# The first chunk of x transposed tile by tile ahead of its norm in a macaron decoder step

## The chip, the cores and the metric

One NeuronCore of a Trainium2 chip runs the whole program; the other cores are idle. The metric is the device time of one execution in microseconds (us). Five engines work side by side, each through its own list of instructions in a fixed order: TensorE (PE in the profile, with its weight loads listed as PEld), VectorE (DVE), ScalarE (ACT), GpSimd (POOL) and SyncE (SP), which here only issues DMAs. An engine whose next instruction waits for a semaphore runs nothing that stands behind it.

## The reference, cut to what matters

The program computes one step of a hybrid recurrent decoder with one layer, for 1024 prompt rows and 32 sample rows of width 1024. The change is in the first half-step, which is a SwiGLU feed-forward block on normalised rows:

```python
def rmsnorm(x, g):
    xf = x.astype(jnp.float32)
    y = xf * lax.rsqrt(jnp.mean(xf * xf, axis=-1, keepdims=True) + EPS)
    return (y * g.astype(jnp.float32)).astype(x.dtype)

def swiglu(x, w_gu, w_down):
    gate, up = jnp.split(x @ w_gu, 2, axis=-1)
    return (jax.nn.silu(gate) * up) @ w_down
...
x = x + 0.5 * swiglu(rmsnorm(x, norm_ffn1[l]), w_ffn1_gu[l], w_ffn1_down[l])
```

A mixer (three kinds of heads behind one input projection) and a second SwiGLU block follow, and a last RMSNorm. The change leaves all of that alone.

## The kernel before, in words

x arrives in nine tiles of 128 rows, in three chunks of three tiles (`CH`: 384, 384 and 288 columns once transposed). The kernel keeps x transposed: `xT[k]` holds columns 128k to 128k+127 of x on the partitions, with the rows of x along the free dimension. A chunk is brought in by `x_chunk(c)`. First `rms_rows` takes the sum of squares of each tile (tiles 0 and 2 on ScalarE, tile 1 on VectorE), one square root (ScalarE), one reciprocal and three scaled identities `dg` (VectorE); three products of `dg` with a matrix of ones (TensorE, "row products" below) spread the reciprocal norms over all partitions, and ScalarE copies them to `F1.row`. Then 24 TensorE transposes (three tiles by eight k) go through PSUM, and ScalarE and VectorE copy the eight results into `xT[k]`, every other one each.

All float32 products are made of three fp32r products: a matrix is split into a high part `h` (a cast on ScalarE) and a low part `l` (a subtraction on VectorE), and each k contributes l·xh, h·xl and h·xh. `raw1(j)` loads the gate and up columns of weight block j, `parts` splits them. `F1.build(0, first=True)` makes the normalised x in blocks: for each k one VectorE product of `xT[k]`, the gain and `row` (`b`), one ScalarE cast (`fh`) and one VectorE subtraction (`fl`); `b11` and `b21` are the first quarter of the rows (264 columns, k 0 to 3 and 4 to 7), `b12` and `b22` the second quarter.

`plain(j, q, ...)` computes block j for quarter q: 24 products for the gate (`pg`), a Silu on ScalarE, 24 products for up (`pu`), a VectorE product `z` and a store. The program text runs `plain(0,0)`, `x_chunk(1)`, `plain(1,0)`, `plain(2,0)`, `x_chunk(2)`, then the small vectors of the later stages (`small_vectors(8, ...)`: nine small loads into `vr`, one transpose, one copy), then `plain` for quarter 1 of blocks 0, 1, 2 and for blocks 20 and 21, and then the long `gate_up` loop, whose first product in the profile is `pb` at L430.

The order on each engine is set by a scheduler, which places the instructions by priorities and by its own idea of durations; `tc.keep_in_program_order` pins an instruction to its place among the other pinned ones. Before the change the squares and the other steps of `rms_rows` are pinned for chunks 1 and 2, and the transposes are pinned nowhere. `AHEAD`, `AHEAD_GU` and `AHEAD_EV` raise priorities. The scheduler opens two PSUM tags of four banks here, "mm" and "aux". The lines that are spoken of:

```python
r0 = raw1(0)
x_chunk(0)
W = {0: [parts(r) for r in r0]}
...
next(b0)
next(b0)
W[1] = [parts(r, pin=tc.keep_in_program_order) for r in r1]
plain(0, 0, W[0], F1, hd1)
x_chunk(1)
plain(1, 0, W[1], F1, hd1)
```

Of the kernel before, what the change touches and what calls it, by code (L numbers as in the profile page):

```python
# [15 lines left out]
AF = mybir.ActivationFunctionType  # L16
# [14 lines left out]
CH = [(0, 384), (384, 384), (768, 288)]  # L31
# [57 lines left out]
def build(ctx, tc, I, O, cdP, cd4):  # L89
    nc = tc.nc  # L90
    pe, act, dve, gps, sp = nc.tensor, nc.scalar, nc.vector, nc.gpsimd, nc.sync
# [17 lines left out]
    def B(name, dt=F32):  # L109
        return blk.tile([P, PITCH], dt, name=name, tag="b")[:, :BW]  # L110

    def ps2(name):
        return pool["pp"].tile([P, 2, 512], F32, name=name, tag="two")

    def ps(tag="aux", name="ps"):
        if pool["gu"]:
            return ps2(name)[:, 0, :]
        return pool["pp"].tile([P, 512], F32, name=name, tag=tag)

    def tm(name, tag, n=384, bufs=None):  # L120
# [8 lines left out]
    idt = cst.tile([P, P], F32, name="idt")  # L129
    make_identity(nc, idt)  # L130
    ones = cst.tile([P, P], F32, name="ones")
    dve.memset(ones, 1.0)
    epsb = cst.tile([P, 1], F32, name="epsb")
# [6 lines left out]
    def tr(out, in_):  # L140
        k = in_.shape[0]
        return pe.transpose(out, in_, idt[:k, :k])


    sm = cst.tile([P, 64], F32, name="sm")
    SMO = {}

    def small_vectors(o, names):
        vr = tm("vr", "sq", P)
        gps.memset(vr, 0.0)  # L150
        n = 0
        for name in names:
            a = I[name]
            src = a.rearrange(("(k p) -> k p", "l (k p) -> (l k) p", "l j (k p) -> (l j k) p")[len(a.shape) - 1], p=P)
            sp.dma_start(vr[n:n + src.shape[0], :], src)
            SMO[name] = o + n
            n += src.shape[0]
        p = ps()
        tr(p[:, :P], vr)
        dve.tensor_copy(sm[:, o:o + n], p[:, :n])  # L160

    def col(name, i):
        return sm[:, SMO[name] + i:SMO[name] + i + 1]
# [7 lines left out]
    def wtile(tag, k, m, dt=F32R):  # L171
        t = ws.tile([P, KT * P], dt, name=tag, tag=tag)
        return t[:, :k * m].rearrange("p (k m) -> p k m", k=k)

    def raw(srcs, nk, m, pin=lambda i: i):
        r = wtile("wr", nk, m, F32)
        k0 = 0
        for s in srcs:
            n = s.shape[0] // P
            pin(sp.dma_start(r[:, k0:k0 + n, :], s.rearrange("(k p) m -> p k m", p=P)))  # L180
            k0 += n
        return r

    def parts(r, e=dve, home=None, pin=lambda i: i):
        h, l = home() if home else (wtile("wh", *r.shape[1:]), wtile("wl", *r.shape[1:]))
        pin(act.copy(h, r))  # L186
        tt(l, r, h, SUB, e)
        return h, l
# [21 lines left out]
    def rel(c, i):  # L210
        return tok(3 * c + i) - CH[c][0]


    def tiles(c):
        return [(i, rel(c, i)) for i in ((0, 1, 2) if c < 2 else (2, 0, 1))]
# [178 lines left out]
    def plain_weights(wgu, j):  # L394
        with tc.high_priority(AHEAD_GU):
            return [parts(raw([wgu[:, o + j * P:o + (j + 1) * P]], KT, P)) for o in (0, FF)]

    def plain(j, q, W, F, hd, step=lambda: None):

        X = [F.f[i, 0] for i in ((0, 1) if q == 0 else (7, 5))]  # L400

        def product(p, u):
            h, l = u
            for k in range(KT):
                xh, xl = (x[:, k % 4] for x in X[k // 4])
                pe.matmul(p, l[:, k], xh, start=k == 0, stop=False)
                pe.matmul(p, h[:, k], xl, start=False, stop=False)
                pe.matmul(p, h[:, k], xh, start=False, stop=k == KT - 1)
            step()

        g, u, z = ps("mm", "pg")[:, :Q], ps("aux", "pu")[:, :Q], tm("z", "s")[:, :Q]
        product(g, W[0])
        with tc.high_priority(AHEAD_EV):
            act.activation(z, g, AF.Silu)
        product(u, W[1])
        with tc.high_priority(AHEAD_EV):
            stt(z, u, 0.5, z, MUL, MUL)
        sp.dma_start(hd[j * P:(j + 1) * P, q * Q:(q + 1) * Q], z)

    def gu(j, W, F, ss, hd, step=lambda: None):  # L420

        ns = len(ss)

        def product(i, t, first):
            h, l = W[i]
            for e, s in enumerate(ss):
                xh, xl = F.f[i, s]
                o = t[:, e]
                for k in range(4):
                    pe.matmul(o, l[:, k], xh[:, k], start=first and k == 0, stop=False, skip_group_check=not first)  # L430
                    pe.matmul(o, h[:, k], xl[:, k], start=False, stop=False, skip_group_check=not first)  # L431
                    pe.matmul(o, h[:, k], xh[:, k], start=False, stop=k == 3, skip_group_check=not first)  # L432
            step()
# [111 lines left out]
    def down7(xT, hd, hf, wd, first):  # L545
        groups = [(2 * i, 2 * i + 1) for i in range(NP7 // 2)]
        F = first

        def product(i, t, W, start):
            h, l = W[i]  # L550
            for s in range(2):
                o = t[:, s, :Q]
                for n, f in enumerate(F):
                    xh, xl = f[i][:, 0, s], f[i][:, 1, s]
                    st, sk = start and n == 0, not start
                    pe.matmul(o, l[:, n], xh, start=st, stop=False, skip_group_check=sk)  # L556
                    pe.matmul(o, h[:, n], xl, start=False, stop=False, skip_group_check=sk)  # L557
                    pe.matmul(o, h[:, n], xh, start=False, stop=n == len(F) - 1, skip_group_check=sk)  # L558
# [129 lines left out]
    xin = []  # L688
# [11 lines left out]
    xT = [B(f"xT{k}") for k in range(KT)]  # L700
# [11 lines left out]
    F1 = Forms(xT, "norm_ffn1")  # L712
    junk, junk2 = B("junk"), B("junk")

    def rms_rows(c, row):

        pin = tc.keep_in_program_order if c else lambda i: i
        xn = xin[3 * c:3 * c + 3]
        c0, n = CH[c]
        ss = tm("ss", "ss", 3)  # L720
        for i in range(3):
            if i != 1:
                pin(act.activation(junk[:, :D], xn[i][:, :D], AF.Square, accum_out=ss[:, i:i + 1]))
            else:
                stt_ = dve.scalar_tensor_tensor
                pin(stt_(out=junk2[:, :D], in0=xn[i][:, :D], scalar=1.0, in1=xn[i][:, :D], op0=MUL, op1=MUL, accum_out=ss[:, i:i + 1]))
        rstd(ss, ss, 1.0 / D)
        dg = tm("dg", "dg", bufs=3)
        p = ps()
        for i, o in tiles(c):  # L730
            tsc(dg[:, i * P:(i + 1) * P], idt, ss[:, i:i + 1], MUL)
            pe.matmul(p[:, o:o + P], ones, dg[:, i * P:(i + 1) * P], start=True, stop=True)
        act.copy(row[:, c0:c0 + n], p[:, :n])

    def x_chunk(c):
        c0, n = CH[c]
        xn = xin[3 * c:3 * c + 3]
        rms_rows(c, F1.row)
        for k in range(KT):
            pk = ps("mm" if k % 2 else "aux")  # L740
            for i, o in tiles(c):
                tr(pk[:, o:o + P], xn[i][:, k * P:(k + 1) * P])
            (act.copy if k % 2 else dve.tensor_copy)(xT[k][:, c0:c0 + n], pk[:, :n])

    small_vectors(0, ["norm_ffn1"])
    w1 = I["w_ffn1_gu"][0]
    hd1 = dr.tile([FF, T], F32, name="hd1")
    hf1 = dr.tile([NP7, 7, P, T], F32, name="hf1")

    raw1 = lambda j: [raw([w1[:, o + j * P:o + (j + 1) * P]], KT, P, tc.keep_in_program_order) for o in (0, FF)]  # L750
    w2_home = lambda: [B("w2", F32R)[:, :D].rearrange("p (k m) -> p k m", k=KT) for _ in range(2)]
    load_x(0)
    r0 = raw1(0)
    x_chunk(0)
    W = {0: [parts(r) for r in r0]}
    load_x(1)
    r1, r2 = raw1(1), raw1(2)
    load_x(2)
    b0 = F1.build(0, first=True)
    next(b0)  # L760
    next(b0)
    W[1] = [parts(r, pin=tc.keep_in_program_order) for r in r1]
    plain(0, 0, W[0], F1, hd1)
    x_chunk(1)
    plain(1, 0, W[1], F1, hd1)
    W[2] = [parts(r, home=w2_home, pin=tc.keep_in_program_order) for r in r2]
    next(b0)
    next(b0)
    plain(2, 0, W[2], F1, hd1)
    x_chunk(2)  # L770
    small_vectors(8, ["norm_mix", "norm_ffn2", "g_ret_norm", "g_mlstm_norm", "w_conv", "b_conv", "b_lru_a", "b_lru_i", "lru_lambda"])
    step = lambda: next(b0, None)
    for j in (0, 1, 2):
        plain(j, 1, W[j], F1, hd1, step)
# [1 line left out]
    step = lambda: next(b1, None)  # L776
    for j in (20, 21):
        u = plain_weights(w1, j)
# [763 lines left out]
    b0 = F2.build(0)  # L1542
# [19 lines left out]
    for j in (0, 20, 21):  # L1562
        u = plain_weights(w2, j)
# [106 lines left out]
```

## Time and profile before

| what | before |
|---|---|
| median of 3 runs | 1993.12 us (1992.91 to 1995.72) |
| the profiled execution's own time | 1990.73 us |
| its span, first to last instruction | 1988.9 us |
| TensorE busy with products | 1947.9 us (98% of the span) |
| VectorE, ScalarE, GpSimd busy | 1378.4, 755.8, 128.1 us |
| first product of `plain` starts | 17.67 us |
| first product of `gate_up` starts | 88.72 us |

A row of the timeline has its start, its length, engine, line, operation, output and inputs, the number of instructions in the row, and in brackets how long the engine had been idle before and for whom. Products are pipelined, so one that is 0.28 us long may start 0.12 us after the one ahead of it: what a product costs is the distance between two starts. [...]

### The profile page before, as it was taken

The numbers are of one execution on the slowest core, as the hardware profiler recorded it, in microseconds if no ns is written. First come the engines' busy times: TensorE is split into PE (matmuls) and PEld (weight loads), VectorE is DVE, ScalarE is ACT, GpSimd is POOL, SyncE is SP. The second block draws the span as 40 slices with busy tenths as digits, with TensorE's granted clock in tenths as the row PEclk, the third lists the DMA queues.
The fourth block names the chain that finished last, engine by engine and source line by source line (L and its number), as shares of the span: only waits on it lengthen the run. The fifth ranks groups of instructions, "written<-read, shape, count | busy, mean of one in ns | idle before, by whom it ended". The sixth has DMA issues, their size and how long they took to land.

```text
span 1988.9 us, 36911 instructions
## 1 busy us (share of the span) xinstructions
PE 1947.9 (98%) x15110; PEld 1912.6 (96%) x15110; DVE 1378.4 (69%) x2575; ACT 755.8 (38%) x1294; POOL 128.1 (6%) x175
## 2 busy tenths in 40 slices
PE   7999999999899999999999999999999999999998
PEld 7999999999899999999999989999999999999997
DVE  6857766665787875556558569986665666578787
ACT  6534443443232363212242324544443444323234
POOL 0000000000000034222112041000000000000000
PEclk9999999999999999999999999999999999999999
DMA  7335875569759432111211262524665556985932
GB/s 253 106 102 200 288 253 186 183 215 365 305 197 348 158 123 76 55 47 51 56 32 38 70 153 68 170 71 162 234 221 201 185 185 210 361 316 199 348 97 88
DMA packets 270927, 347.03 MB, mean 174 GB/s; under 512 B 17015, under 2 KB 219014, under 8 KB 270758
## 3 DMA queue, kind: packets, MB, share of 16 engines
q1 hardware_dynamic: 270758, 344.67, 50.4%
q8 instruction: 119, 1.95, 0.4%
q14 instruction: 50, 0.41, 0.1%
HBM read 224.82 MB, written 119.80 MB: 173 GB/s over the span
## 4 chain that ended last, share of the span: by engine, by line
PE 88%; DVE 6%; ACT 2%; DMA 2%; issue 1%; POOL 1%; DVEq 0%; SPq 0%; POOLq 0%; ACTq 0%
PE pb L430 8%; PE pb L431 8%; PE pb L432 8%; PE pj L199 4%; PE pj L201 4%; PE pj L200 4%; PE pc L430 4%; PE pc L431 4%; PE pc L432 4%; PE db L556 4%; PE db L557 4%; PE db L558 3%; PE dc L557 2%; PE dc L556 2%; PE dc L558 2%; PE pa L430 2%
## 5 line engine op out<-in xcount | busy, mean ns | idle before, releaser
L123 DVE TENSOR_TENSOR wl<-wr,wh 128x1024 fp32r<-128x1024 f32 (+3 forms) x442 | 362.7, 842 | 177.1 <-ACT wh L186 170.8
L186 ACT CAST wh<-wr 128x1024 fp32r<-128x1024 f32 (+2 forms) x242 | 229.9, 951 | 436.9 <-PE pj L201 146.1
L430 PE MATMUL pb<-fh,wl 128*128 128x264 f32 x1312 | 375.2, 286 | 2.8 <-DVE z L126 1.9
L431 PE MATMUL pb<-fl,wh 128*128 128x264 f32 x1312 | 372.4, 284 | 0.0
L432 PE MATMUL pb<-fh,wh 128*128 128x264 f32 x1312 | 369.7, 282 | 0.0
L430 PEld LDWEIGHTS pb<-fh,wl 128*128 128x128 f32 x1312 | 246.3, 188 | 7.6 <-DVE z L126 2.1
L431 PEld LDWEIGHTS pb<-fl,wh 128*128 128x128 f32 x1312 | 246.6, 188 | 0.0
L432 PEld LDWEIGHTS pb<-fh,wh 128*128 128x128 f32 x1312 | 246.4, 188 | 0.0
L556 PE MATMUL db<-hf,wl 128*128 128x264 f32 x640 | 183.4, 287 | 10.3 <-DVE wl L123 9.8
L199 PE MATMUL pj<-xh,wl 128*128 128x384 f32 (+1 forms) x576 | 187.8, 326 | 0.0
L201 PE MATMUL pj<-xh,wh 128*128 128x384 f32 (+1 forms) x576 | 187.1, 325 | 0.0
L123 DVE TENSOR_TENSOR wr<-wr 128x512 f32<-128x512 f32 (+1 forms) x336 | 176.1, 561 | 15.7 <-DMA wr<-in_w_ffn_gu 10.2
L200 PE MATMUL pj<-xl,wh 128*128 128x384 f32 (+1 forms) x576 | 185.8, 323 | 0.0
L557 PE MATMUL db<-hf,wh 128*128 128x264 f32 x640 | 182.9, 286 | 0.0
L430 PE MATMUL pc<-fh,wl 128*128 128x264 f32 x640 | 181.9, 284 | 0.0
L558 PE MATMUL db<-hf,wh 128*128 128x264 f32 x640 | 181.9, 284 | 0.0
L431 PE MATMUL pc<-fl,wh 128*128 128x264 f32 x640 | 181.8, 284 | 0.0
L432 PE MATMUL pc<-fh,wh 128*128 128x264 f32 x640 | 180.5, 282 | 0.0
L191 ACT CAST wh<-wr 128x256 fp32r<-128x256 f32 (+1 forms) x200 | 87.3, 490 | 187.1 <-PE dc L558 108.5
L556 PEld LDWEIGHTS db<-hf,wl 128*128 128x128 f32 x640 | 121.5, 190 | 12.2 <-issue 10.5
L558 PEld LDWEIGHTS db<-hf,wh 128*128 128x128 f32 x640 | 121.4, 190 | 0.0
L557 PEld LDWEIGHTS db<-hf,wh 128*128 128x128 f32 x640 | 121.1, 189 | 0.0
(460 smaller groups left out, 4742.2 us busy)
## 6 DMA issues: line engine op xcount, KB each, us to landing
hf<-hf SPq DMA_DIRECT2D x280, 528.0 KB
wr<-in_w_ffn_gu SPq DMA_DIRECT2D x104, 512.0 KB
hr<-hd SPq DMA_DIRECT2D x44, 528.0 KB
wr<-in_w_ffn_down SPq DMA_DIRECT2D x44, 512.0 KB
spill<-xT SPq DMA_DIRECT2D x24, 528.0 KB
xT<-spill SPq DMA_DIRECT2D x24, 528.0 KB
wr<-in_w_in SPq DMA_DIRECT2D x24, 512.0 KB
hd<-u SPq DMA_DIRECT2D x36, 264.0 KB
```

The costliest lines, as they stand in the source:

```text
L123: tt = lambda o, a, b, op, e=dve: e.tensor_tensor(out=o, in0=a, in1=b, op=op)
L186: pin(act.copy(h, r))
L191: act.copy(h, x)
L199: pe.matmul(p, l[:, ku, m0:m0 + P], xh[:, c0:c0 + n], start=i == 0, stop=False)
L200: pe.matmul(p, h[:, ku, m0:m0 + P], xl[:, c0:c0 + n], start=False, stop=False)
L201: pe.matmul(p, h[:, ku, m0:m0 + P], xh[:, c0:c0 + n], start=False, stop=i == last)
L430: pe.matmul(o, l[:, k], xh[:, k], start=first and k == 0, stop=False, skip_group_check=not first)
L431: pe.matmul(o, h[:, k], xl[:, k], start=False, stop=False, skip_group_check=not first)
L432: pe.matmul(o, h[:, k], xh[:, k], start=False, stop=k == 3, skip_group_check=not first)
L556: pe.matmul(o, l[:, n], xh, start=st, stop=False, skip_group_check=sk)
L557: pe.matmul(o, h[:, n], xl, start=False, stop=False, skip_group_check=sk)
L558: pe.matmul(o, h[:, n], xh, start=False, stop=n == len(F) - 1, skip_group_check=sk)
```

## The change

Seven edits, all in the first 60 us of the program:

- Before anything else nine products of a matrix of ones are issued (`warm_up`), five ahead of the transpose of the first gain vector and four behind it; their results are not used.
- Chunk 0 no longer goes through `x_chunk` but through the new generator `x_first`: each tile's eight transposes are issued as the tile lands, into eight PSUM tiles held at once; all eight copies into `xT` are on ScalarE.
- The first weight block is split by halves (k 0 to 3, k 4 to 7), cast and low part in turn with the copies, all pinned.
- `plain(0,0)` (`both=True`) takes the products of gate and up by halves: gate k 0 to 3, up k 0 to 3, gate k 4 to 7, up k 4 to 7.
- The loads of x's second chunk and of block 1 are issued right behind those of block 0, block 2's load behind them.
- The transposes of chunks 1 and 2 are pinned to program order.
- The nine loads of the later small vectors are pinned, behind the third store of `z`.

```diff
+    def small_vectors(o, names, pin=lambda i: i, pin_all=lambda i: i):
...
+            pin(sp.dma_start(vr[n:n + src.shape[0], :], src))
...
+        pin_all(tr(p[:, :P], vr))
+        pin_all(dve.tensor_copy(sm[:, o:o + n], p[:, :n]))
...
         g, u, z = ps("mm", "pg")[:, :Q], ps("aux", "pu")[:, :Q], tm("z", "s")[:, :Q]
-        product(g, W[0])
+        if both:
+            for i in range(2):
+                for p, w in ((g, W[0]), (u, W[1])):
+                    product(p, w, range(4 * i, 4 * i + 4))
+        else:
+            product(g, W[0])
         with tc.high_priority(AHEAD_EV):
             act.activation(z, g, AF.Silu)
-        product(u, W[1])
+        if not both:
+            product(u, W[1])
...
             for i, o in tiles(c):
-                tr(pk[:, o:o + P], xn[i][:, k * P:(k + 1) * P])
+                tc.keep_in_program_order(tr(pk[:, o:o + P], xn[i][:, k * P:(k + 1) * P]))
...
+    def warm_up(n):
+        p = ps("mm")
+        for _ in range(n):
+            pin(pe.matmul(p[:, :P], ones, ones, start=True, stop=True))
+
+    def x_first(rg, ru):
+        c0, n = CH[0]
+        ss = tm("ss", "ss", 3)
+        pk = [ps("mm" if k % 2 else "aux") for k in range(KT)]
+        g, u = ((wtile("wh", KT, P), wtile("wl", KT, P)) for _ in range(2))
+        half = (slice(0, 4), slice(4, 8))
...
+        def copy(k):
+            pin(act.copy(xT[k][:, c0:c0 + n], pk[k][:, :n]))
+        for i, o in tiles(0):
+            x = xin[i][:, :D]
+            if i != 1:
+                pin(act.activation(junk[:, :D], x, AF.Square, accum_out=ss[:, i:i + 1]))
+            else:
+                pin(dve.scalar_tensor_tensor(out=junk2[:, :D], in0=x, scalar=1.0, in1=x, op0=MUL, op1=MUL, accum_out=ss[:, i:i + 1]))
+            for k in range(KT):
+                pin(tr(pk[k][:, o:o + P], x[:, k * P:(k + 1) * P]))
+        pin(act.activation(ss, ss, AF.Sqrt, bias=epsb, scale=1.0 / D))
+        pin(dve.reciprocal(ss, ss))
+        dg = tm("dg", "dg", bufs=3)
+        for i, o in tiles(0):
+            pin(tsc(dg[:, i * P:(i + 1) * P], idt, ss[:, i:i + 1], MUL))
+        cast(g, rg, 0)
+        low(g, rg, 0)
+        copy(1)
+        copy(0)
+        copy(2)
+        p = ps("mm")
+        for i, o in tiles(0):
+            pin(pe.matmul(p[:, o:o + P], ones, dg[:, i * P:(i + 1) * P], start=True, stop=True))
+        pin(act.copy(F1.row[:, c0:c0 + n], p[:, :n]))
+        copy(3)
+        yield
+        cast(u, ru, 0)
+        low(u, ru, 0)
+        copy(4)
+        copy(5)
+        cast(g, rg, 1)
+        low(g, rg, 1)
+        copy(6)
+        copy(7)
+        cast(u, ru, 1)
+        yield g, u
+        low(u, ru, 1)
+        yield
...
+    warm_up(5)
+    small_vectors(0, ["norm_ffn1"], pin, pin)
+    warm_up(4)
...
     r0 = raw1(0)
-    x_chunk(0)
-    W = {0: [parts(r) for r in r0]}
     load_x(1)
-    r1, r2 = raw1(1), raw1(2)
+    r1 = raw1(1)
+    b0 = F1.build(0, first=True)
+    xf = x_first(*r0)
+    next(xf)
+    next(b0)
+    W = {0: next(xf)}
+    next(b0)
+    next(xf)
+    r2 = raw1(2)
     load_x(2)
-    b0 = F1.build(0, first=True)
-    next(b0)
-    next(b0)
     W[1] = [parts(r, pin=tc.keep_in_program_order) for r in r1]
-    plain(0, 0, W[0], F1, hd1)
+    plain(0, 0, W[0], F1, hd1, both=True)
```

The scheduler's orders change with it. On TensorE, between the last product of `plain(0,0)` and `plain(1,0)`, where chunk 1 is brought in, the order before was this (`ps<-idt,xin` is a transpose of x, `ps<-dg,ones` a row product, which waits for chunk 1's norm, `pg` and `pu` are products of gate and up):

```order
L408 MATMUL pu<-fh,wh 128x264
L142 MATMUL ps<-idt,xin 128x128 x11
L406 MATMUL pg<-fh,wl 128x264
...
L408 MATMUL pg<-fh,wh 128x264
L732 MATMUL ps<-dg,ones 128x128 x3
L142 MATMUL ps<-idt,xin 128x128 x12
L406 MATMUL pu<-fh,wl 128x264
```

And at the same place it is now:

```order
L408 MATMUL pu<-fh,wh 128x264
L738 MATMUL ps<-dg,ones 128x128 x3
L142 MATMUL ps<-idt,xin 128x128 x24
L406 MATMUL pg<-fh,wl 128x264
L407 MATMUL pg<-fl,wh 128x264
```

The row products moved ahead of all 24 transposes of the chunk and of all 24 gate products of block 1; before, twelve transposes (one of them far ahead) and the 24 gate products stood in front of them.

Where chunk 2 comes in, behind the up products of block 2 (`w_404` and `w_405` before, `w_419` and `w_420` now), the order on TensorE before was:

```order
L408 MATMUL pu<-fh,w_404 128x264
L142 MATMUL ps<-idt,xin 128x128 x12
L406 MATMUL pg<-fh,wl 128x264
...
L407 MATMUL pg<-fl,wh 128x264
L732 MATMUL ps<-dg,ones 128x128 x3
L142 MATMUL ps<-idt,xin 128x128 x9
```

And now:

```order
L408 MATMUL pu<-fh,w_419 128x264
L738 MATMUL ps<-dg,ones 128x128 x3
L142 MATMUL ps<-idt,xin 128x128 x24
L142 MATMUL ps<-idt,vr 128x128
L406 MATMUL pg<-fh,wl 128x264
```

Here too nothing is left in front of the row products; twelve transposes and the products of quarter 1 stood there before.

On ScalarE the piece from the first casts of block 1 (`wh<-wr`) to the square root of chunk 1's norm (`ss<-ss,epsb`) was, before:

```order
L186 CAST wh<-wr 128x1024
L414 ACT_TABLE_LOAD
L414 ACTIVATE z<-pg 128x264
L186 CAST wh<-wr 128x1024
L723 ACTIVATE junk,ss<-xin 128x1024
L743 COPY xT_86<-ps 128x384
L723 ACTIVATE junk,ss<-xin 128x1024
L743 COPY xT_88<-ps 128x384
L207 ACT_TABLE_LOAD
L207 ACTIVATE ss<-ss,epsb 128x3
```

And now:

```order
L186 CAST wh<-wr 128x1024
L419 ACT_TABLE_LOAD
L419 ACTIVATE z<-pg 128x264
L186 CAST wh<-wr 128x1024
L729 ACTIVATE junk,ss<-xin 128x1024 x2
L207 ACT_TABLE_LOAD
L207 ACTIVATE ss<-ss,epsb 128x3
```

The piece is the same but for two copies of transposed x, which are behind the square root now.

## Rows read from the trace of the kernel before

**Rows 1.** The page: span, busy time and share of each engine, and the shares of the chain that ended last.

```profile
span 1988.9 us, 36911 instructions
PE 1947.9 (98%) x15110; PEld 1912.6 (96%) x15110; DVE 1378.4 (69%) x2575; ACT 755.8 (38%) x1294; POOL 128.1 (6%) x175
PE 88%; DVE 6%; ACT 2%; DMA 2%; issue 1%; POOL 1%; DVEq 0%; SPq 0%; POOLq 0%; ACTq 0%
```

**Rows 2.** The timeline of TensorE in the first 26 us: start, length, line, operation, tiles, count, idle time before.

```profile
5.43 0.47 PE L142 MATMUL ps<-idt,xin 128*128 128x128 f32 x1 [1.94 <-DMA xin<-in_x_prompt]
...
10.19 1.65 PE L732 MATMUL ps<-dg,ones 128*128 128x128 f32 x6 [0.86 <-DVE dg L124]
11.63 3.83 PE L142 MATMUL ps<-idt,xin 128*128 128x128 f32 x17
17.67 0.59 PE L406 MATMUL pg<-fh,wl 128*128 128x264 f32 x1 [2.20 <-ACT fh L191]
...
22.11 0.42 PE L407 MATMUL pg<-fl,wh 128*128 128x264 f32 x1
22.33 0.42 PE L408 MATMUL pg<-fh,wh 128*128 128x264 f32 x1
...
25.80 0.28 PE L408 MATMUL pu<-fh,wh 128*128 128x264 f32 x1
25.92 0.28 PE L406 MATMUL pu<-fh,wl 128*128 128x264 f32 x1
```

**Rows 3.** The timeline of TensorE from 26 to 51 us, the same columns.

```profile
26.30 1.36 PE L142 MATMUL ps<-idt,xin 128*128 128x128 f32 x11
...
31.12 0.94 PE L732 MATMUL ps<-dg,ones 128*128 128x128 f32 x6 [0.40 <-DVE dg L124]
31.89 1.69 PE L142 MATMUL ps<-idt,xin 128*128 128x128 f32 x12
...
36.31 0.29 PE L406 MATMUL pg<-fh,w 128*128 128x264 f32 x1
...
47.29 0.94 PE L732 MATMUL ps<-dg,ones 128*128 128x128 f32 x6
```

**Rows 4.** The timeline of ScalarE: the first row copy and a pair of xT copies, the piece from block 1's first cast to the square root of chunk 1, and a half-sized cast further on.

```profile
9.22 0.30 ACT L207 ACTIVATE ss<-ss,epsb 128x3 f32<-128x3 f32 x1
11.91 0.47 ACT L733 COPY row<-ps 128x384 f32<-128x384 f32 x1
12.28 0.86 ACT L743 COPY xT<-ps 128x384 f32<-128x384 f32 x2
...
21.69 0.82 ACT L191 CAST fh<-b 128x264 fp32r<-128x264 f32 x2 [1.02 <-DVE b L126]
22.41 1.04 ACT L186 CAST wh<-wr 128x1024 fp32r<-128x1024 f32 x1
...
28.95 1.28 ACT L207 ACT_TABLE_LOAD   x1
30.24 0.30 ACT L207 ACTIVATE ss<-ss,epsb 128x3 f32<-128x3 f32 x1
...
43.28 1.09 ACT L324 CAST fh<-b 128x1056 fp32r<-128x1056 f32 x1
...
87.90 0.61 ACT L186 CAST wh<-wr 128x512 fp32r<-128x512 f32 x1
```

**Rows 5.** The timeline of VectorE: the pieces of the first block, the norms' scaled identities, and the steps around chunk 2's norm.

```profile
17.89 1.12 DVE L123 TENSOR_TENSOR fl<-b,fh 128x264 fp32r<-128x264 f32 x3
30.78 0.68 DVE L124 TENSOR_SCALAR dg<-idt,ss 128x128 f32<-128x128 f32 x3
44.40 1.26 DVE L123 TENSOR_TENSOR fl<-b,fh 128x1056 fp32r<-128x1056 f32 x1
45.57 1.25 DVE L123 TENSOR_TENSOR t<-b,b 128x1056 f32<-128x1056 f32 x1
46.74 0.17 DVE L208 RECIPROCAL ss<-ss 128x3 f32<-128x3 f32 x1
46.95 0.68 DVE L124 TENSOR_SCALAR dg<-idt,ss 128x128 f32<-128x128 f32 x3
53.33 0.43 DVE L126 SCALAR_TENSOR_TENSOR z<-pu,z 128x264 f32<-128x264 f32 x1
70.02 4.12 DVE L126 SCALAR_TENSOR_TENSOR b<-xT,sm,row 128x264 f32<-128x264 f32 x10
90.34 1.89 DVE L123 TENSOR_TENSOR wr<-wr 128x512 f32<-128x512 f32 x3
```

**Rows 6.** Busy time of each engine by stretches (stretch and its length, PE, PEld, DVE, ACT, POOL with counts, granted TensorE clock, DMA share, GB/s), around a short stall in the mixer.

```profile
1177.00:1180.20 3.20, 1.38 (x12) 1.17 (x12) 2.73 (x15) 1.04 (x4) 1.05 (x2) 0.99 0.02 4
1180.20:1183.60 3.40, 3.40 (x19) 3.40 (x18) 3.15 (x10) 0.00 (x0) 0.19 (x1) 0.50 0.75 126
```

**Rows 7.** Issues by SyncE: the first and the last of the nine small vectors that are moved (start, length with waits).

```profile
4.25 3.34 SPq L155 DMA_DIRECT2D vr<-in_norm_mix  x1
...
11.23 0.25 SPq L155 DMA_DIRECT2D vr<-in_lru_lambda  x1
```

**Rows 8.** The first product of `gate_up` in TensorE's timeline, with its wait.

```profile
88.72 0.39 PE L430 MATMUL pb<-fh,wl 128*128 128x264 f32 x1 [1.88 <-DVE z L126]
```

More of the change, by code (lines that the diff above doesn't have):

```diff
@@ L146, in build @@
     SMO = {}
-    def small_vectors(o, names):
+    def small_vectors(o, names, pin=lambda i: i, pin_all=lambda i: i):
         vr = tm("vr", "sq", P)
@@ L154, in small_vectors @@
             src = a.rearrange(("(k p) -> k p", "l (k p) -> (l k) p", "l j (k p) -> (l j k) p")[len(a.shape) - 1], p=P)
-            sp.dma_start(vr[n:n + src.shape[0], :], src)
+            pin(sp.dma_start(vr[n:n + src.shape[0], :], src))
             SMO[name] = o + n
@@ L158, in small_vectors @@
         p = ps()
-        tr(p[:, :P], vr)
-        dve.tensor_copy(sm[:, o:o + n], p[:, :n])
+        pin_all(tr(p[:, :P], vr))
+        pin_all(dve.tensor_copy(sm[:, o:o + n], p[:, :n]))
     def col(name, i):
@@ L396, in plain_weights, with plain, product @@
             return [parts(raw([wgu[:, o + j * P:o + (j + 1) * P]], KT, P)) for o in (0, FF)]
-    def plain(j, q, W, F, hd, step=lambda: None):
+    def plain(j, q, W, F, hd, step=lambda: None, both=False):
         X = [F.f[i, 0] for i in ((0, 1) if q == 0 else (7, 5))]
-        def product(p, u):
+        def product(p, u, ks=range(KT)):
             h, l = u
-            for k in range(KT):
+            for k in ks:
                 xh, xl = (x[:, k % 4] for x in X[k // 4])
@@ L741, in x_chunk, with cast, low @@
             for i, o in tiles(c):
-                tr(pk[:, o:o + P], xn[i][:, k * P:(k + 1) * P])
+                tc.keep_in_program_order(tr(pk[:, o:o + P], xn[i][:, k * P:(k + 1) * P]))
             (act.copy if k % 2 else dve.tensor_copy)(xT[k][:, c0:c0 + n], pk[:, :n])
-    small_vectors(0, ["norm_ffn1"])
+    def warm_up(n):
[8 more added lines that the diff above has]
+        half = (slice(0, 4), slice(4, 8))
+        def cast(w, r, i):
+            pin(act.copy(w[0][:, half[i]], r[:, half[i]]))
+        def low(w, r, i):
+            pin(tt(w[1][:, half[i]], r[:, half[i]], w[0][:, half[i]], SUB))
+        def copy(k):
[36 more added lines that the diff above has]
+        yield
@@ L746, in build @@
+    pin = tc.keep_in_program_order
+    warm_up(5)
+    small_vectors(0, ["norm_ffn1"], pin, pin)
+    warm_up(4)
     w1 = I["w_ffn1_gu"][0]
@@ L770, in build @@
     x_chunk(2)
-    small_vectors(8, ["norm_mix", "norm_ffn2", "g_ret_norm", "g_mlstm_norm", "w_conv", "b_conv", "b_lru_a", "b_lru_i", "lru_lambda"])
+    small_vectors(8, ["norm_mix", "norm_ffn2", "g_ret_norm", "g_mlstm_norm", "w_conv", "b_conv", "b_lru_a", "b_lru_i", "lru_lambda"], pin)
     step = lambda: next(b0, None)
```

## Prediction

> **What bounds the kernel now.** I read the page first: TensorE is busy for 98% of the span and carries 88% of the chain that ended last [rows 1]. So the only things that can move the time are what TensorE waits for and how fast its clock runs. The change touches the first 60 us alone; every engine's order behind that is the old one. So I read the timelines of that stretch, TensorE's first. The first real product stands at 17.67 us, behind the norm, 24 transposes and the first splits [rows 2]. From there TensorE hardly stops: up to 53 us the largest wait is 0.40 us, at 31.12, for chunk 1's scaled identities [rows 3]. [...] ScalarE and VectorE [rows 4, 5] make what TensorE eats here, so I then asked where their chains end in the new order, engine by engine.
>
> **The change part by part.**
>
> *Start of the first products: a gain.* The square root of chunk 0 stands at 9.22 [rows 4]; nothing in the change makes it earlier. Behind it ScalarE now casts half a block (0.61) and copies three xT (0.38 apart, from 0.86 for two) [rows 4], until 11.1. The row copy may start then, if the row products are ready. At the low clock, 24 transposes from 5.43 on, one every 0.213 (17 took 3.83), and six row instructions end at about 11.9 [rows 2]; at the high clock by 11. So the row copy is at 11.1 to 12.05, against 11.91. But now three xT wait beside it. Copy 0.47, the product b 0.4 to 0.5, cast 0.41: the first product starts at 12.5 to 13.5, some 4 to 5 us earlier than 17.67.
>
> *The first block: VectorE sets the pace.* Eight b at 0.40 (ten took 4.12), eight fl at 0.35 (three took 1.12) and three half-block low parts at 0.60 (three sums of that size took 1.89) make 7.8 us [rows 5]. Twice VectorE waits some 0.5 for one cast (0.41), and once 0.8 to 0.9 behind ScalarE's two half casts and two copies (1.9 us against 0.95 of its own work). That is 9.8 us from the first b (11.6 to 12.6): the last low part is ready at 21.4 to 22.4, and the last 12 up products end at 22.9 (0.12 each) to 25.4 (0.22). Before, TensorE left this block at 26.30 [rows 3]. Gain so far: 1 to 3.4 us.
>
> *Chunk 1: a wait of 4 to 5 us that was covered before.* The scaled identities of chunk 1 hang on a chain on ScalarE: cast, table load, Silu, cast, two squares, table load, square root. Before, it ran from 22.41 to the identities at 30.78, 8.4 us [rows 4, 5]. Two copies (0.8) leave it, so 7.6. It starts when the last fh cast is done, 1.2 us before the last low part: 20.2 to 21.2. Identities at 27.8 to 28.8, row products 0.34 later as at 30.78 and 31.12, so 28.1 to 29.1. Before, eleven transposes (26.30) and block 1's 24 gate products ran on TensorE meanwhile, and the wait left was 0.40 [rows 3]. In the new order the row products stand first, and the 24 transposes and all 48 products of block 1 behind them. TensorE waits from 22.9 (25.4) to 28.1 (29.1): 5.2 or 3.7 us.
>
> *What the wait does to the clock.* In the mixer, a stretch of 3.2 us with 1.38 us of products was followed by 3.40 us in which the granted clock was 0.50 [rows 6]. The waits here are emptier, so I take the low level for 24 of the 30 instructions behind them: 24 at 0.213 and 6 at 0.12 make 5.8 us, against 3.7 at the high level and 6.4 with all low. [...]
>
> *Block 2 and chunk 2: a second wait.* From 28.1: 5.8, then 48 products at 0.12 (5.8): block 2's first product at 39.7, against 36.31 [rows 3], late by 3.4 (bounds: 1.3 with the high clock, 5 with the low). Block 2 ends at 45.6. Chunk 2's identities now need, in this order: block 2's z on VectorE (0.43, ready when TensorE ends), two b (0.8), a 1056-column cast (1.08), its low part (1.17, from 44.40 to 45.57), a subtraction (1.17), reciprocal and identities (0.21), row product (0.34) [rows 4, 5]. With 0.1 to 0.2 for each hand-over that is 5.7 us in which TensorE has nothing in front: row products at 51.3. Before, they started at 47.29 with no wait [rows 3], since the products of quarter 1 filled the time. This wait is the same 5.7 whatever the first one was.
>
> *To the end of `plain(0,1)`.* 31 instructions (row products, 24 transposes, the small vectors' transpose) 6.0, 48 products 5.8: its up products end at 63.2. Before, z followed them at 53.33 [rows 5], so they ended at 53.2. TensorE is 10.0 us late, with bounds of 5.7 (clock high throughout: 2 x 2.2 less) and 12.
>
> *Edits at nothing.* The nine small loads now stand behind the third z (about 46). Before, they took from 4.25 to 11.48, 7.2 us [rows 7]; at that pace they are issued by 53 and land by 55, and TensorE wants them at 57: 2 us of cover, and if it is gone, `plain(0,1)` waits as long as they are late. The loads of chunk 1 and block 1 are issued earlier than before; they stand behind block 0's in one queue, and the squares that read chunk 1 come four instructions down the chain above.
>
> *What comes back.* `gate_up` began at 88.72 after a wait of 1.88 us for VectorE's last z [rows 8]. VectorE was behind then. In the new run it has waited for TensorE, not the other way round, and by the order has 33 us of work left behind the z of `plain(0,1)` (7 block low parts and 12 steps of 1056 columns at 1.15, 16 b, 4 half sums, 7 z at 0.35), as much as TensorE, which took from 53.2 to 86.8. So 0 to 1.9 comes back; I take 1.0. From there on the order is the old one and nothing runs on an outer clock, so the rest shifts as a whole.
>
> **Sum.** +3.4 at block 2, 5.7 of wait and 0.9 more in slow transposes to +10.0, less 1.0: +9.0 us. On the profiled execution's 1990.73 that is 1999.7; that execution is 2.4 us under the median of the runs shown, so on 1993.12 it is **2002 us**, 0.45% slower.
>
> [...]
>
> **The rivals.**
> 1. *The waits are there, but cost less*: the clock stays up through both, or the order leaves more ahead than I count. For it: in rows 6 the drop came after a stretch that was 43% busy, and no earlier stall in this stretch tests it. Then +5.7 at 53 us, less 1 to 1.9: +3.8 to +4.7, so 1997 to 1998. Against: waits of 4 and 5.7 us are longer than anything there.
> 2. *The gain is kept: faster.* Mechanism: chunk 1's identities are ready when block 0's products end. That needs ScalarE's two squares and square root some 4 us sooner than summed, by about 24 us: the Silu, which waits for the last gate product, stands in front of them. If that holds, TensorE keeps the 3.4 us, and chunk 2's wait shrinks too; up to 4.6 us with the late clock rise gone: 1988.5 to 1990. Against: the eight instructions of the chain stand in a fixed order, each with a measured length.
> 3. *Nothing moves*: VectorE's backlog sets the start of `gate_up` (1.88 us of wait in rows 8), and lateness on TensorE is swallowed there. It can swallow 1.9 us, and with the high clock and short chains, 3.8 less another 1 or 2: 1993 to 1996. Against: rows 8 give no more room than 1.9.
>
> **How the numbers follow.** Forecast (+6 to +12, 1999 to 2005): 0.66. Rival 1: 0.14. Rival 3: 0.11. Rival 2: 0.09. The range reaches from rival 1's lower half to past the forecast's upper bound, 1996 to 2006. A difference below 0.2% (4 us) can't be told from none here. Slower by more than that: the forecast and nearly all of rival 1, 0.79. Within: rival 3 and the rest of 1, and half of rival 2, 0.14. Faster: 0.07.
>
> **What would show it.** In the new profile the first product should start at 12.5 to 13.5; row products of chunk 1 (L738) should show a wait of 4 to 5 us for `dg`, those of chunk 2 one near 5.7; transposes behind both should run 0.21 us apart at first; the first product of `gate_up` should be near 97.7. If TensorE's waits for `dg` are under 1 us, or `gate_up` starts before 90 us, the prediction is wrong; if both waits are there but transposes run 0.12 apart, only the size is.

## The result, and the profile after

The changed kernel takes 2004.89 us in the median of 4 runs (2002.76 to 2006.60), against 1993.44 for the kernel before beside it: a ratio of 1.0050, 95% interval 1.0035 to 1.0065. It is slower, by 11.45 us. The forecast was 2002, with a range of 1996 to 2006. The profiled execution took 2004.93 us, its span is 2003.1.

The page of the kernel after, the lines that answer to [rows 1]:

```profile
span 2003.1 us, 36955 instructions
PE 1955.2 (98%) x15128; PEld 1918.6 (96%) x15128; DVE 1376.1 (69%) x2573; ACT 758.7 (38%) x1300; POOL 127.8 (6%) x175
```

TensorE's share is the same 98%: a loss of 11 us can't be seen in shares. It is seen in the timeline of TensorE, at the places of [rows 2] and [rows 3]. Columns are start, length, engine, line, operation, output and inputs, count, and in brackets the idle time before and for whom:

```profile
10.54 0.94 PE L794 MATMUL ps<-dg,ones 128*128 128x128 f32 x6 [1.42 <-ACT xT L772]
13.01 0.59 PE L406 MATMUL pg<-fh,wl 128*128 128x264 f32 x1 [1.54 <-ACT fh L191]
...
23.36 0.28 PE L408 MATMUL pu<-fh,wh 128*128 128x264 f32 x1
28.82 1.65 PE L738 MATMUL ps<-dg,ones 128*128 128x128 f32 x6 [5.17 <-DVE dg L124]
...
33.91 0.37 PE L406 MATMUL pg<-fh,wl 128*128 128x264 f32 x1
...
39.80 0.32 PE L406 MATMUL pg<-fh,w 128*128 128x264 f32 x1
...
51.65 1.62 PE L738 MATMUL ps<-dg,ones 128*128 128x128 f32 x6 [5.86 <-DVE dg L124]
...
57.33 0.27 PE L142 MATMUL ps<-idt,vr 128*128 128x128 f32 x1
57.36 0.37 PE L406 MATMUL pg<-fh,wl 128*128 128x264 f32 x1
...
98.12 0.29 PE L436 MATMUL pb<-fh,wl 128*128 128x264 f32 x1
```

The first product stands at 13.01 (before 17.67) and block 0 is done at 23.5 (before 26.30). Then the row products of chunk 1 wait 5.17 us, where [rows 3] has 0.40; those of chunk 2 wait 5.86 us, where [rows 3] has none. `gate_up` begins at 98.12 instead of 88.72 [rows 8]: 9.4 us late. TensorE's granted clock in the same stretches (stretch and its length, busy time of PE, PEld, DVE, ACT, POOL with counts, granted clock, DMA share, GB/s):

```profile
12.00:18.80 6.80, 5.67 (x22) 5.10 (x23) 5.63 (x13) 5.60 (x14) 0.00 (x0) 0.50 0.83 285
18.90:25.70 6.80, 4.28 (x27) 3.31 (x26) 5.58 (x12) 5.72 (x10) 0.00 (x0) 1.00 0.62 187
25.70:32.50 6.80, 3.68 (x17) 3.68 (x18) 2.26 (x7) 3.46 (x6) 0.00 (x0) 0.50 1.06 327
32.50:49.60 17.10, 13.30 (x111) 13.09 (x109) 11.28 (x19) 10.17 (x15) 0.00 (x0) 1.00 0.33 97
49.60:56.40 6.80, 4.75 (x22) 4.78 (x23) 5.52 (x10) 4.18 (x7) 0.00 (x0) 0.50 0.10 38
56.40:63.00 6.60, 6.60 (x57) 6.60 (x56) 5.64 (x11) 3.97 (x6) 0.00 (x0) 1.00 1.02 414
```

Each wait has a stretch at 0.50 that begins inside it and reaches past it: 25.70 to 32.50 for the wait from 23.65 to 28.82, 49.60 to 56.40 for the one from 45.79 to 51.65. In this trace two 264-column products start 0.22 us apart where the granted clock is 0.50 (14.32 and 14.54), and 0.12 apart where it is 1.00 (22.28 and 22.40); these are the low and the high clock below. The chain that ends in the first wait, on ScalarE:

```profile
20.72 1.04 ACT L186 CAST wh<-wr 128x1024 fp32r<-128x1024 f32 x1
21.78 1.28 ACT L419 ACT_TABLE_LOAD   x1
23.07 0.39 ACT L419 ACTIVATE z<-pg 128x264 f32<-128x264 f32 x1
23.36 1.04 ACT L186 CAST wh<-wr 128x1024 fp32r<-128x1024 f32 x1
24.30 1.06 ACT L729 ACTIVATE junk<-xin 128x1024 f32<-128x1024 f32 x1
...
25.48 1.06 ACT L729 ACTIVATE junk<-xin 128x1024 f32<-128x1024 f32 x1
...
26.64 1.28 ACT L207 ACT_TABLE_LOAD   x1
27.94 0.30 ACT L207 ACTIVATE ss<-ss,epsb 128x3 f32<-128x3 f32 x1
```

ScalarE has no gap there from the first row to the last: the square root at 27.94 comes as soon as what is queued ahead of it is done, and TensorE had nothing in front of the row products from 23.5 on. The chain that ends in the second wait is VectorE's own. Block 2's up products end at 45.8, and VectorE then goes from the `z` to the scaled identities without a gap:

```profile
46.31 0.42 DVE L126 SCALAR_TENSOR_TENSOR z<-pu,z 128x264 f32<-128x264 f32 x1
...
47.45 1.22 DVE L732 SCALAR_TENSOR_TENSOR junk<-xin 128x1024 f32<-128x1024 f32 x1
...
48.67 1.26 DVE L123 TENSOR_TENSOR fl<-b,fh 128x1056 fp32r<-128x1056 f32 x1
49.85 1.25 DVE L123 TENSOR_TENSOR t<-b,b 128x1056 f32<-128x1056 f32 x1
...
51.22 0.68 DVE L124 TENSOR_SCALAR dg<-idt,ss 128x128 f32<-128x128 f32 x3
```

From about 100 us on both kernels run in the same order. Compared instruction by instruction, the kernel after is 9.9 us late at 982 us and 14.2 us at the end of this execution. Most of what comes in addition, 3.7 us, comes between 1160 and 1210 us, and the experiments below return to it.

### The profile page after: what moved, and what is told of

It is laid out like the page before. It is cut to its first block, busy times and chain, and to the rows that moved or that the text cites. A ratio compares the mean times of both kernels' runs of the same rounds, so it can differ in the third digit from the quotient of the medians.

```text
span 2003.1 us, 36955 instructions
## 1 busy us (share of the span) xinstructions
PE 1955.2 (98%) x15128; PEld 1918.6 (96%) x15128; DVE 1376.1 (69%) x2573; ACT 758.7 (38%) x1300; POOL 127.8 (6%) x175
## 4 chain that ended last, share of the span: by engine, by line
PE 86%; DVE 7%; DMA 3%; ACT 2%; issue 1%; POOL 1%; SPq 0%; DVEq 0%; POOLq 0%; ACTq 0%
PE pb L436 8%; PE pb L437 8%; PE pb L438 8%; PE pj L199 4%; PE pj L200 4%; PE pj L201 4%; PE pc L437 4%; PE pc L436 4%; PE pc L438 4%; PE db L562 4%; PE db L563 3%; PE db L564 3%; PE dc L563 2%; PE pa L436 2%; PE pa L437 2%; PE dc L564 2%
## 5 line engine op out<-in xcount | busy, mean ns | idle before, releaser
L191 ACT CAST wh<-wr 128x256 fp32r<-128x256 f32 (+1 forms) x200 | 87.5, 490 | 189.8 <-PE dc L564 109.1
```

Source lines behind the costliest of these rows:

```text
L191: act.copy(h, x)
```

## The experiments

Start of `gate_up` in the profiled execution, and the ratio of times to the kernel before. The changed kernel was profiled in two executions, which start `gate_up` 1.4 us apart; a smaller difference between two profiles shows nothing by itself.

| kernel | `gate_up` starts, us | ratio, 95% interval |
|---|---|---|
| before | 88.72 | 1 |
| after | 98.12 | 1.0050 (1.0035 to 1.0065) |
| after, run again | 99.55 | 1.0057 (1.0044 to 1.0070) |
| after, transposes unpinned | 87.86 | 0.9994 (0.9983 to 1.0006) |
| before, transposes pinned | 102.19 | 1.0075 (1.0058 to 1.0091) |
| after, row products behind the transposes | 84.38 | 0.9975 (0.9964 to 0.9986) |
| the same for chunk 1 alone | 91.84 | 1.0017 (1.0003 to 1.0031) |
| the same for chunk 2 alone | 89.92 | 1.0009 (0.9999 to 1.0019) |
| after, waits filled with products | 94.01 | 1.0022 (1.0012 to 1.0031) |
| after, chunk 1's squares first | 98.22 | 1.0050 (1.0037 to 1.0064) |
| rows behind, without warm-up | 84.26 | 0.9978 (0.9969 to 0.9987) |
| before, row products behind the transposes | 85.49 | 0.9992 (0.9982 to 1.0002) |

**Which line loses the time.** Two runs change nothing but whether the transposes are pinned. In the first, those of chunks 1 and 2 are no longer pinned in the changed kernel:

```diff
-                tc.keep_in_program_order(tr(pk[:, o:o + P], xn[i][:, k * P:(k + 1) * P]))
+                tr(pk[:, o:o + P], xn[i][:, k * P:(k + 1) * P])
```

> The changed kernel, but the transposes of chunks 1 and 2 are pinned nowhere, as before the change. TensorE's order then has 12 transposes of chunk 1 spread through block 0 and all 24 gate products of block 1 ahead of chunk 1's row products, and 12 transposes and 41 products of quarter 1 ahead of chunk 2's. Theory (the pinned transposes put the row products in front, and TensorE waits there for the norm): both waits for dg fall from 5.17 and 5.86 us to under 1 us, the low clock behind them goes, gate_up starts between 84 and 89 us instead of 98.1, and the run takes 1989 to 1994 us, 11 to 15 less than the changed kernel. Rival (block 0's new order, with all copies on ScalarE and the products by halves, makes the norm chains late): the waits are turned into others, gate_up starts after 95 us and the run takes over 2000 us.

The time was 1995.20 against 1995.36 before; `gate_up` starts at 87.86. The loss is gone, though one wait is only halved and the clock still falls behind it (0.50 from 30 to 33 us). In this kernel's TensorE timeline:

```profile
27.03 0.28 PE L408 MATMUL pg<-fh,wh 128*128 128x264 f32 x1
30.09 1.65 PE L738 MATMUL ps<-dg,ones 128*128 128x128 f32 x6 [2.78 <-DVE dg L124]
```

The theory's "under 1 us" was wrong there: the 12 transposes that now run inside block 0 bring their xT copies and the Silu of block 1 ahead of chunk 1's square root on ScalarE, which moves from 27.94 to 29.21. The second kernel puts the same line, pinned, into the kernel before, with nothing else of the change.

> The kernel before, with the transposes of x_chunk pinned and nothing else of the change. TensorE's order has the row products of chunks 1 and 2 right behind blocks 0 and 2, as in the changed kernel. Theory (this one line carries the loss): row products of chunk 1 wait 3 to 5 us, those of chunk 2 5 to 6.5 us, each followed by the lower clock; gate_up starts at 97 to 101 us and the run takes 2001 to 2007 us, as slow as the changed kernel or slower, since the earlier first product is missing. Rival (the new first block carries it): waits under 2 us and 1992 to 1996 us.

It took 2010.43 us, with `gate_up` at 102.19, both above the expected ranges, and its TensorE timeline has the same two waits (the pin holds for chunk 0 too there; its first product stands at 17.45, before at 17.67):

```profile
30.39 1.47 PE L732 MATMUL ps<-dg,ones 128*128 128x128 f32 x6 [5.12 <-DVE dg L124]
...
53.09 1.62 PE L732 MATMUL ps<-dg,ones 128*128 128x128 f32 x6 [5.86 <-DVE dg L124]
```

So this one line is enough for the whole loss. It loses more here than the change as a whole: block 0 ends 1.6 us later than in the changed kernel, and in front of `gate_up` TensorE waits 2.5 us for a `z`, where the changed kernel has no wait.

**Is it the pinning, or what stands in front?** The transposes stay pinned, but the row products are written behind them (`rms_rows` yields ahead of its `dg` loop, `x_chunk` resumes it at its end):

```diff
         dg = tm("dg", "dg", bufs=3)
+        yield
         p = ps()
...
-        rms_rows(c, F1.row)
+        rr = rms_rows(c, F1.row)
+        next(rr)
         for k in range(KT):
...
+        next(rr, None)
```

> The changed kernel with its pinned transposes, but the row products of chunks 1 and 2 are written behind the chunk's transposes, so that 24 transposes and 24 (25) gate products stand in front of them on TensorE. Theory (it is not the pinning but what stands in front of the row products): the waits for dg fall below 1.5 us in the first place and to nothing in the second, gate_up starts between 84 and 89 us, and the run takes 1989 to 1994 us, like the run with unpinned transposes within 2 us. Rival (pinned transposes cost by themselves, as they need PSUM tiles and copies in a fixed order): waits for the xT copies appear in place of those for dg, and the run stays above 1998 us.

```profile
23.54 2.78 PE L142 MATMUL ps<-idt,xin 128*128 128x128 f32 x24
29.47 0.94 PE L739 MATMUL ps<-dg,ones 128*128 128x128 f32 x6 [0.24 <-DVE dg L124]
33.96 0.39 PE L406 MATMUL pg<-fh,w 128*128 128x264 f32 x1 [0.67 <-DVE w L123]
39.88 2.78 PE L142 MATMUL ps<-idt,xin 128*128 128x128 f32 x24
46.06 0.84 PE L739 MATMUL ps<-dg,ones 128*128 128x128 f32 x6
```

The scaled identities are no earlier than in the changed kernel (its row products start at 29.47, there at 28.82), but TensorE now works until then. The waits of 5.17 and 5.86 us shrink to 0.24 and none; the granted clock is 1.00 throughout from 18.9 to 84 us; the kernel takes 1989.69 us, 5.7 us less than the kernel before beside it. The expectation had it within 2 us of the run with unpinned transposes, which took 1995.20. The transposes are pinned here too, so pinning by itself is not what costs.

**What each wait costs.** The same edit for one chunk alone:

> The changed kernel with the row products of chunk 1 alone written behind the transposes; those of chunk 2 stay in front of theirs. Theory (two waits that cost each for itself, the second the same whatever becomes of the first): no first wait, block 2's first product at 34.0 as in the run with both moved instead of 39.8, the second wait still 5.5 to 6.2 us at about 46, the low clock behind it, gate_up at 91.5 to 94, and the run some 6 us faster than the changed kernel. Rival (with the first wait gone, VectorE is behind and the second wait grows by as much): second wait of 8 us or more, gate_up after 95.

> The changed kernel with the row products of chunk 2 alone written behind the transposes. Theory: first wait 5.2 us and low clock behind it as in the changed kernel, block 2's first product at 39.5 to 41, no second wait, gate_up at 90 to 92, and the run some 7 to 8 us faster than the changed kernel. Rival (TensorE, let through at chunk 2, catches up with VectorE and waits further on): no wait for dg, but waits over 3 us for z, fl or wl between 50 and 95 us, gate_up after 94.

With chunk 1 alone moved, TensorE still has, at chunk 2:

```profile
45.86 1.62 PE L739 MATMUL ps<-dg,ones 128*128 128x128 f32 x6 [5.85 <-DVE dg L124]
```

With chunk 2 alone moved, the first wait is 5.17 us and there is no second. Against 84.38 with both moved, the first wait is worth 89.92 - 84.38 = 5.5 us and the second 91.84 - 84.38 = 7.5, together 13.0 of the 13.7 us between 84.38 and 98.12. The 0.7 that is left is within what two executions differ by, and the ratios of times add up as well: 0.0034 and 0.0042 above 0.9975 make 0.0076, where the changed kernel has 0.0075 and 0.0082. Neither rival holds.

**What of that is the clock.** The waits are filled with products whose result nobody reads, 40 behind block 0 and 44 behind block 2:

```diff
+        if fill:
+            f = ps("mm", "pf")[:, :Q]
+            for _ in range(fill):
+                pe.matmul(f, W[1][1][:, 7], X[1][0][:, 3], start=True, stop=True)
```

> The changed kernel with extra products whose result is not used in the place of the two waits: 40 behind block 0 and 44 behind block 2, each 128x264 like those of the blocks. Nothing that the kernel computes is changed. It leaves the norm chains as they are and takes away only the idleness. Theory (the idleness costs twice, once as wait and once as 6.8 us of lower clock behind it): waits under 1 us, granted clock 1.00 behind both, the 27 or so instructions behind each 0.12 to 0.14 us apart instead of 0.21, gate_up 3.5 to 4.5 us earlier than 98.1, and the run takes 3.5 to 4.5 us less than the changed kernel, 2000 to 2002 us. Rival (the clock behind the waits doesn't matter, since VectorE's chains set the pace there): the same waits for the next step, gate_up at 97 to 98 us, the time of the changed kernel within 1 us.

```profile
28.86 0.94 PE L742 MATMUL ps<-dg,ones 128*128 128x128 f32 x6 [0.31 <-DVE dg L124]
29.63 2.78 PE L142 MATMUL ps<-idt,xin 128*128 128x128 f32 x24
32.17 0.37 PE L406 MATMUL pg<-fh,wl 128*128 128x264 f32 x1
...
49.83 0.94 PE L742 MATMUL ps<-dg,ones 128*128 128x128 f32 x6 [0.42 <-DVE dg L124]
...
53.25 0.37 PE L406 MATMUL pg<-fh,wl 128*128 128x264 f32 x1
```

The row products start where they did (28.86 for 28.82), so nothing of the chain is better. But from there to the next gate product it is 3.3 us instead of 5.1, and 3.4 instead of 5.7 at chunk 2, at a granted clock of 1.00 in both places, where the changed kernel has 0.63 and 0.58. That is 4.1 us, all of it still there at `gate_up` (94.01 for 98.12). Some 4 of the 13.7 us are therefore the clock behind the waits; the other 9.6 are what the two waits, 11.0 us together, still cost at `gate_up`.

**What the first wait hangs on.** Block 1's splits are written behind chunk 1's norm, so that ScalarE squares sooner:

```diff
-        rms_rows(c, F1.row)
+        rms_rows(c, F1.row)
+        mid()
...
-    W[1] = [parts(r, pin=tc.keep_in_program_order) for r in r1]
...
-    x_chunk(1)
+    x_chunk(1, lambda: W.update({1: [parts(r, pin=tc.keep_in_program_order) for r in r1]}))
```

> The changed kernel, but the splits of block 1's weights (two casts on ScalarE, two subtractions on VectorE) are written behind chunk 1's norm and ahead of its transposes, so that ScalarE goes from the Silu of block 0 straight to chunk 1's squares. TensorE's order stays as in the changed kernel. Theory (the wait of 5.17 us is the rest of ScalarE's chain: cast, table load, Silu, cast, two squares, table load, square root): two casts of 0.95 us leave the chain, so the scaled identities are ready at 26.1 to 27.0 instead of 28.5, the row products wait 2.7 to 3.5 us, the second wait stays near 5.9, gate_up starts at 95.5 to 97, and the run takes 1 to 2.5 us less than the changed kernel. Rival (the wait is for something else: chunk 1's load, VectorE's queue): the wait stays at 5 us or more.

ScalarE, and TensorE below it:

```profile
24.44 0.19 ACT L729 ACTIVATION_READ_ACCUMULATOR junk<-xin 128x1 f32 x1
25.30 1.28 ACT L207 ACT_TABLE_LOAD   x1 [0.68 <-DVE junk L732]
```
```profile
27.48 1.65 PE L738 MATMUL ps<-dg,ones 128*128 128x128 f32 x6 [3.94 <-DVE dg L124]
28.92 4.84 PE L142 MATMUL ps<-idt,xin 128*128 128x128 f32 x24
33.52 0.37 PE L406 MATMUL pg<-fh,wl 128*128 128x264 f32 x1
```

The wait fell from 5.17 to 3.94 us, not to 3. ScalarE did finish its squares 2.0 us sooner (24.63 for 26.63), but then waits 0.68 us for VectorE's square of the middle tile, which stands behind the `z` of block 0. That is a second chain: in the changed kernel it ends at 25.33, only 1.3 us ahead of ScalarE's squares. And most of the gain was lost at once. The row products and transposes took 6.0 us (27.48 to 33.52) where they had taken 5.1, as more of them ran at the low clock (0.53 on the mean of this stretch, 0.63 in the changed kernel). The second execution of the changed kernel took 6.0 us there as well, so this run does not show that the shorter wait is the reason. `gate_up` starts at 98.22, and the time is that of the changed kernel. A shorter chain brought no time here; work in front of the wait did.

**What the new first block is worth.** From the kernel with the row products behind, the nine warm-up products are taken out; and the kernel before gets the row products behind, its chunk 0 as it was.

> The kernel with the row products written behind the transposes (gate_up at 84.4 there), without the nine warm-up products. Theory (the warm-up is worth next to nothing, since VectorE paces block 0): transposes of chunk 0 run 0.21 us apart instead of 0.13, the first product starts at 13.2 to 13.7 instead of 13.04, gate_up at 84.6 to 85.9, the run within 1.5 us of the one with warm-up. Rival (the clock then stays low through block 0 and the transposes of chunk 1, so that the warm-up carries the gain): gate_up at 86.5 to 88, 2 to 4 us more.

> The kernel before with its chunk 0 as it was, and for chunks 1 and 2 the transposes pinned and the row products written behind them, as in the run at 1989.7 us. Theory (the new first block is worth some 4 us, and the place of the row products only keeps it): no wait for dg over 0.5 us, gate_up starts at 87.5 to 89.5 as before, and the run is within 2 us of the kernel before. Rival (the gain of that run comes from the row products standing further back): gate_up at 84 to 86, the run 3 to 5 us faster than the kernel before.

Without warm-up the first product is even at 12.94 and `gate_up` at 84.26, and the ratio is 0.9978 for 0.9975: in this kernel the warm-up is worth nothing that shows. The kernel before with the edit starts its first product at 17.10, 4.1 us later than the changed one, but `gate_up` only 1.1 us later (85.49), and its time is 0.9992 of before. So of the 4 us that the first product gains, 1.1 us are left when `gate_up` begins. In the new first block VectorE sets the end: its last low part is done at 21.92 in the kernel with the row products behind, and the 12 products that wait for it end at 23.5. `gate_up` itself is 3.2 us earlier than before; of these, 1.9 are the wait for `z` in [rows 8], which is gone, and about 1.5 stand in block 0, whose code is untouched (its `z` at 25.04 for 26.57): in this execution products stand 0.12 apart from 20.5 on, in [rows 2] only from 23 (the late clock rise that rival 2 prices). That part looks like the execution's and not the edit's, which one profile of each can't settle. Without it the new first block would be worth 2.6 us, and the times say as much: 1989.81 us without warm-up and 1992.53 for this kernel, run side by side, are 2.7 us apart, though the intervals of their ratios overlap. The clock in the kernel with the edit:

```profile
17.00:20.40 3.40, 3.30 (x13) 3.09 (x14) 3.40 (x11) 2.08 (x6) 0.00 (x0) 0.51 1.11 349
20.40:24.70 4.30, 4.30 (x36) 4.30 (x36) 3.16 (x6) 3.55 (x6) 0.00 (x0) 0.99 1.13 372
```

The expectation gave 87.5 to 89.5 and missed for both reasons. `gate_up` is where the rival had it, the time where the theory had it.

No run takes out the products by halves, the earlier loads or the pinned small loads alone.

**The time behind 1160 us.** The changed kernel once more:

> The changed kernel once more, for its time beside the others and a second profile. Theory (the change costs some 10 us in the first 100, and the 4 us that the first profile shows in the mixer belong to that execution): gate_up at 98.1 again within 0.3, the lag behind the kernel before at 982 us 9.9 again, the lag at the end anywhere from 6 to 15, and 1.004 to 1.0065 of the time before. Rival (the mixer part belongs to the change): lag at the end 13 to 15 again, with the same second low-clock stretch near 1200 us.

It took 2005.84 us; the lag at 982 us is 10.4 (9.9 in the first profile), the one at the end some 13. `gate_up` starts at 99.55, outside the expected 0.3: both waits are the same (5.18 and 5.85), but the low stretch lies further behind them, and from the row products to the next gate product it takes 6.0 and 6.2 us instead of 5.1 and 5.7:

```profile
23.60:28.80 5.20, 0.05 (x1) 0.00 (x0) 3.20 (x7) 4.58 (x7) 0.00 (x0) 0.88 1.00 324
28.80:34.00 5.20, 5.17 (x24) 5.17 (x25) 1.77 (x5) 1.44 (x3) 0.00 (x0) 0.50 1.02 266
```

In the mixer the first profile had two low stretches, where [rows 6] has one:

```profile
1176.00:1179.40 3.40, 3.40 (x17) 3.35 (x16) 2.83 (x9) 2.00 (x5) 3.40 (x4) 0.50 0.03 9
...
1199.90:1203.30 3.40, 3.40 (x17) 3.38 (x16) 3.12 (x18) 0.48 (x1) 1.27 (x2) 0.50 0.89 290
```

The second profile has one, near 1200, and loses 1.7 us there. Its lag at the end fits the theory (6 to 15) and, within 0.1 us, the rival (13 to 15), so this run alone doesn't decide between them. Other kernels help. Those that are no slower than before and still have pinned transposes (rows behind, with and without warm-up, and the kernel before with the edit) lose some 2 us or more against the trace of before at this same place; the one with unpinned transposes loses nothing. Both executions without a loss were quick ones: 1990.73 us with a median of 1993.44 for the kernel before, 1991.29 with one of 1995.20 for the unpinned one. And in the medians this part doesn't show. Against the kernel before beside it, the kernel with the rows behind is 5.7 us faster (lag at 982 us: -4.0), the one without warm-up 4.6 faster (-2.2), the one with filled waits 4.4 slower (5.1), and the kernel before with pinned transposes 15.1 slower (15.2). So, to within 2.4 us, what a kernel gains or loses is there by 982 us, and the mixer part most likely belongs to the single execution.

## Why the prediction was right, step by step

- *First product at 12.5 to 13.5*: 13.01. *End of block 0 at 22.9 to 25.4, gain 1 to 3.4*: 23.5, gain 2.8 (the late bound adds up to 25.0: 22.4 and 12 products at 0.22). VectorE took 9.9 us from the first b to the last low part, 9.8 were summed. The early end of the ranges, 1 us, was the author's estimate for a high clock in chunk 0's transposes, and no run shows it: with the row products behind, the 24 transposes take 3.67 us with the warm-up and 4.58 without, and the first product starts at 13.04 and 12.94.
- *Chunk 1: row products at 28.1 to 29.1, wait 3.7 to 5.2*: 28.82 and 5.17. The chain on ScalarE was summed right; that VectorE's square ends only 1.3 us ahead of ScalarE's was not seen, and would have been needed to price a shorter chain.
- *Slow transposes, 5.8 us for 30 instructions (3.7 to 6.4)*: 5.1 and, at chunk 2, 5.7 in the first profile, 6.0 and 6.2 in the second. That 24 of the 30 run at the low clock, 5.1 us, was the author's estimate; in the first profile the low stretches end 3.7 and 4.75 us behind the start of the row products. The filler run shows 3.3 and 3.4 at the high clock, so rival 1, the clock up through both waits, would have been 4.1 us less; it was priced at 4.4.
- *Block 2's first product at 39.7, second row products at 51.3 after a wait of 5.7*: 39.80, 51.65, 5.86. That 39.7 came out so close is luck: the row products started 0.7 us later than the 28.1 that the sum began with, and the 30 instructions behind them took 0.7 less. The chain of the second wait is the one that was listed; VectorE's square of chunk 2 was left out of it, but runs beside ScalarE's cast (47.57 to 48.64) and costs nothing. The 0.1 to 0.2 for each hand-over was the author's estimate; where a cast waits for VectorE's `t`, done at 51.10, it starts at 51.13. *The second wait is the same whatever the first was*: 5.85 with the first one removed.
- *Up products of `plain(0,1)` end at 63.2*: the next gate product starts at 63.24. *1.0 us comes back, `gate_up` at 97.7*: 0.6 came back, 98.12, but as the sum of two terms. The whole wait of 1.88 us in [rows 8] is gone. Against it stand 11 gate products of `plain(1,1)`, 1.3 us at 0.12, which the kernel before had run by 53.1 and the new order had not by 63.2; the prediction did not count them. That the two nearly cancel is luck as well.
- *The nine small loads at nothing, issued by 53*: they went faster than the pace of [rows 7], the last at 49.71 to 50.24, and the transpose of `vr` at 57.33 has no wait:

```profile
47.19 0.30 SPq L155 DMA_DIRECT2D vr<-in_norm_mix  x1
...
49.71 0.53 SPq L155 DMA_DIRECT2D vr<-in_lru_lambda  x1
```

- *From there on the rest shifts as a whole*: true to 982 us (9.9), not behind it in this execution. The sum was a little too small: +9.0 was predicted, and medians differ by 11.45. The lag at 982 us, 9.9 and 10.4, accounts for 0.9 to 1.4 of the missing 2.4; the rest lies within the interval of the ratio (7 to 13 us) and isn't assigned to a cause.
- *The table load*: as in [rows 4], it takes 1.28 us at 26.64, and the square root follows 1.30 us after its start. Rivals 2 and 3 are out: no early identities, and no more swallowed than the 1.9 us of [rows 8].

Why one pinned line does so much: TensorE kept to the order of its products here. During the wait of 5.17 us no product ran, although the 24 transposes behind the row products needed only x, and in the run with the row products behind they ran from 23.54.

## What to carry to other kernels

Before pinning, ask what the pinned instructions stand behind: an instruction that waits for a long chain belongs behind all work that is ready, not in front of it. Waits of 5.2 and 5.9 us on TensorE cost 5.5 and 7.5 us here, since the granted clock fell to 0.50 during them and what came next ran slowly, 5.1 and 5.7 us instead of 3.3 and 3.4; shortening the chain by 1.2 us brought nothing, filling the waits with useful work 13.7 us at `gate_up`. And a first product 4 us earlier is worth only what the engine that paces the block (VectorE here) leaves of it: 1.1 us by the profiles, 2.7 by the times.

## What was not expected

Products that compute nothing, put into the waits, made the kernel faster: 4.1 us at `gate_up`, and a ratio of 1.0022 against 1.0050. And the same waits do not always cost the same: in two executions of the same kernel they were 5.2 and 5.9 us, but the low clock lay differently behind them (until 32.50 and 56.40 in the first, still at 34.00 and 58.00 in the second), and the pieces behind the two waits took 1.4 us longer in the second: `gate_up` moved from 98.12 to 99.55.
